# Hybrid decoder step on one core: partial sums of the second gated projection loaded with their gates, mixed forms in three places, and other numbers of staging places at the changes of passes

## The chip, the cores and the metric

The kernel runs on one core of a Trainium2 chip. The metric is the device time of one launch in microseconds (us). Three runs of the kernel before took 2620.25, 2620.29 and 2623.68 us; their median is 2620.29 us.

## The reference

One layer of a decoder is computed in float32 for 1024 prompt tokens and 8 sample tokens, 1032 columns in all, with a model width of 2048.

```
proj = rmsnorm(x, g_pre) @ w_in          # 2048 -> 10240: q k v za ub zb ga gb
ya   = (retention(q, k, v) * silu(za)) @ w_pa          # 1024 -> 2048
y    = gelu(s5(ub));  y = y * sigmoid(y @ w_glu + b)   # 1024 -> 1024
yb   = (y * silu(zb)) @ w_pb                           # 1024 -> 2048
merged = sigmoid(ga) * ya + sigmoid(gb) * yb
out    = x + rmsnorm(merged @ w_out, g_post)           # 2048 -> 2048
```

The states of the retention and of the S5 branch are outputs too; the change does not touch them.

## The kernel before

**Arithmetic.** Activations lie transposed: 128 features on the partitions, tokens along the free axis. Every float32 operand is split into a high and a low part (`whi`/`wlo` for weights, two halves of a tile for activations), and a product is three matmuls. The big projections go by a Winograd form of Strassen's scheme: two blocks of output rows and two halves of the columns are made from seven block products instead of eight. One *step* is one pair of output row blocks, and it has seven *products* n = 0 to 6, run by `product(g)` (L907), where g counts products through the whole program. Product n takes an activation *form* n, one of `FORMS = ("u1", "t2", "v1", "t3", "t1", "t4", "v2")` (L751): u1, v1 and v2 are plain quarters of the input, the t-forms are sums and differences of quarters. Four contraction blocks i = 0 to 3 make 28 form tiles for each pass.

**Passes.** After the passes over `w_in` come five more: `glu` (4 steps, from step SG), `pa` (8 steps, from SA), `pb` (8 steps, from SB), and `w_out` in two halves of its contraction, `o0` (8 steps, from SO) and `o1` (8 steps, from SP). In `o0` and `o1` the forms cover only columns 384 to 1031, 324 for each half; columns 0 to 383 are done last, in plain blocks (the matmuls of L1736), here called the *last stage*. `pa` is the first gated projection: its output times the gate `sga_d` is written to `pap_d` as a partial sum. `pb` is the second: its output times `sgb_d`, plus `pap_d`, is `merged`, written to `mg_d`, which `o0`, `o1` and the last stage read.

**What sets the order.** The code is written as one loop over products; each product is followed by its evacuation (`evac_p` L1453, `evac_o` L1549), by actions put at a product number with `at(g, ...)` (run by `late_work`, L1281), and by one `slot()` (L172) that runs a background generator up to its next `yield`. A scheduler then orders each engine's instructions, and may move a load ahead of where it is written. The engines run their own lists strictly in order. A DMA that an engine issues stands in that engine's list: if it has to wait (for data, or for a buffer), all that is behind it on that engine waits too. SyncE loads weights into `wr`; `prep(g + 2)` (L880) makes the weight tile of a product two products ahead: sums `wraw` on VectorE, then `whi` on ScalarE, then `wlo` on VectorE.

**Evacuation in `pb`.** ScalarE copies product 0 to a tile `p`; VectorE makes `u` tiles and the four results `st` (product 2), `u` (4), `p` (5), `u` (6), and multiplies each by its gate `zz`, which ScalarE's queue loaded two products before (`load_z`, L1423). Then `gated` (L1429) has GpSimd issue a DMA that adds `pap_d` into the tile in SBUF (L1450), and `LAG` = 4 products later a DMA that stores the tile to `mg_d` (L1451). There are two buffers of each kind of tile, one in use by this step and one by the step before.

**Change of passes.** `transition` (L1301) fills the forms of the next pass while the last two steps of the present pass run. With q the number of products since two steps before the new pass, it issues two loads `stg` at q = 0, 1, 2 and 3 (8 places, `stg_open(8)`), and from q = 3 to 19 it splits forms (`unstage`, L859: ScalarE's cast at L259, VectorE's difference), one for each product up to q = 6 and then two, and issues one more load into each place set free. So the four tiles of form n are split by q = 6 + 2n, and product n of the new pass is q = 14 + n.

**Mixed forms for `w_out`.** `forms_o(kh, wait)` (L1480) makes the t-forms of `o0` (from SB + 4) and of `o1` (from SO): for i = 0 to 3 it loads two row blocks of `mg_d`, does four VectorE operations in place, and stores both tiles to `fo_d`. It has two pairs of tiles, so the loads of i = 2 and 3 wait until the stores of i = 0 and 1 have landed.

**The last stage.** `load_m` and `split_m` (L1528, L1531) bring columns 0 to 383 of `mg_d`, four row blocks ahead. A row of `g_post`, spread over all partitions (1 MB, L1702), and the first block of x (1 MB, L1703) are loaded by GpSimd's queue right after the last product of `o1` in the text; `evac_c` (L1705) uses them at the end of each quarter of the last stage.

Of the kernel before, what the change touches and what calls it, by code (L numbers as in the profile page):

```python
# [18 lines left out]
D = 2048  # L19
# [60 lines left out]
def emit(ctx, tc, I, O):  # L80
# [854 lines left out]
    def at(g, f):  # L935
        due.setdefault(g, []).append(f)
# [360 lines left out]

    def stg_open(bufs):
        opened["stg"], opened["stgp"] = popen("stg3", "left", bufs)

    def transition(g, base, kind, eng=P):  # L1301

        q = g - 7 * base
        n = moved.setdefault(kind, [0, 0])
# [5 lines left out]
        if 0 <= q < 4:  # L1310
            load(eng)
            load(eng)
# [110 lines left out]
    def load_z(s, name):  # L1423
        kind, p = steps[s]
        r, c = AT[name]
        zq[name] = zz_tile()
        A.dma_start(zq[name], {"glu": zy_d, "pa": sga_d, "pb": sgb_d}[kind][2 * p + r, :, HT * c:HT * c + HT])

    def gated(g, name, t, ps=None):  # L1429
# [17 lines left out]
        if kind == "pa":  # L1447
            P.dma_start(pap_d[m, :, cols], t)
        else:
            P.dma_start(t, pap_d[m, :, cols], accum_op=ALU.add)  # L1450
            at(g + LAG, lambda: P.dma_start(mg_d[m, :, cols], t))  # L1451
# [28 lines left out]
    def forms_o(kh, wait):  # L1480
# [3 lines left out]
        def ld(i):  # L1484
            if i < 2:
                w[i] = act.tile([128, 2, TOK], F32, name=f"a{(6, 4)[kh] + i}")
            t[i] = w[i % 2][:, 0, 0:SW], w[i % 2][:, 1, 0:SW]
            for x, k in zip(t[i], (8 * kh + i, 8 * kh + 4 + i)):
                P.dma_start(x, mg_d[k, :, TA:TOK])

        for i in range(4):
            if i % 2 == 0:
                if i:
                    yield
                ld(i)
                if i:
                    yield
                ld(i + 1)
                for _ in range(wait):
                    yield  # L1500
            u, v = t.pop(i)
# [7 lines left out]
            P.dma_start(fo_d[kh, 1, i], v)  # L1509
            yield  # L1510

    flat_ = {}
# [15 lines left out]
    def load_m(m):  # L1528
        P.dma_start(spare(m), mg_d[m, :, 0:TA])
# [126 lines left out]
    for s in range(SG, len(steps)):  # L1656
# [3 lines left out]
        if s == SA + 1:  # L1660
            fx_open()
            bg.append(make_forms(yb_d, fb_d))
        if s == SB + 4:
            bg.append(forms_o(0, 2))
        if s in (SG + 2, SB - 2, SB + 6, SP - 2):
            drain()
            stg_open(8)
        if s == SO:
            zstack.close()
            bg.append(forms_o(1, 3))  # L1670
        if s == SO + 1:
# [6 lines left out]
        for n in range(7):  # L1678
# [15 lines left out]
            if s == len(steps) - 1:  # L1694
                for m in range(4) if not n else (n - 1,):
                    at(g, lambda m=m, n=n: split_m(m) if n else load_m(m))
            late_work(g)
# [3 lines left out]
    gb = flat(1, "gb")[:, 0:D]  # L1701
    P.dma_start(gb, bass.AP(tensor=I["g_post_row"].tensor, offset=I["g_post_row"].offset, ap=[[0, 128], [1, D]]))  # L1702
    P.dma_start(x_of(0), I["xB"][0])  # L1703

# [19 lines left out]
    for g in range(4):  # L1724
# [4 lines left out]
        for st in todo_:  # L1729
            for k, c in st:  # L1730
# [6 lines left out]
                if k == KD - 1:  # L1737
                    evac_c(g, c, ps[c])
            now[0] += 1
            if rest:  # L1740
                with ExitStack() as after:
# [87 lines left out]
```

## Time and profile before

| what | value |
|---|---|
| median of three runs | 2620.29 us |
| the profiled execution's own time | 2619.01 us |
| its span, first to last instruction | 2617.1 us |
| TensorE (PE) busy | 2565.9 us, 98% |
| VectorE (DVE), ScalarE (ACT), GpSimd (POOL) busy | 1983.2, 971.5, 784.4 us |
| `pb` ends, `o0` begins | 2249.70 us |
| `o1` ends, the last stage begins | 2466.16 us |

PE is the engine that is nearly always busy, so what counts is where it is not, and where its matmuls run slower than elsewhere. An "x" count in a table by stage is the number of instructions that touch the stage; with one kind of matmul it tells how much of the work got done in it. In rows of waits, "A <- B: total, times, longest" says that A stood idle until B released it. PEclk is the granted clock of TensorE as a share of full speed.

### The profile page before, as it was taken

The page shows a single profiled execution, that of the slowest core. Times are in us where ns is not written, and L with a number is a line of the kernel's source. Part 1 is how long each engine was busy: PE and PEld are TensorE (multiplying, and loading weights), DVE is VectorE, ACT ScalarE, POOL GpSimd, SP SyncE. Part 2 cuts the span into 40 slices and gives each one's busy share as a digit, 9 for nine tenths or more (in the row PEclk, how much of TensorE's full clock was granted, in tenths as well). Part 3 has the DMA queues.
Part 4 walks back from the last instruction along what each step waited for, and adds up shares of the span by engine and source line. Part 5 has one row for each costly group of instructions (what it writes and reads, how often), then busy time and mean ns, then how long its engine had stood idle before and what let it go on. Part 6 is the DMA issues. An engine that isn't in the chain of part 4 may idle for free.

```text
span 2617.1 us, 52507 instructions
## 1 busy us (share of the span) xinstructions
PE 2565.9 (98%) x19948; PEld 2518.0 (96%) x19948; DVE 1983.2 (76%) x4159; ACT 971.5 (37%) x1747; POOL 784.4 (30%) x1300
## 2 busy tenths in 40 slices
PE   9999999999999999999999999999999998799998
PEld 8999999999999999999999999999999998799976
DVE  6655988889889877558877766668886866788875
ACT  6113233333323324343333444346532422345532
POOL 0103322222222222333244444335221323523320
PEclk9999999999999999999999999999999999999999
DMA  5886434434444447888879888889786879957784
GB/s 192 265 267 209 151 115 127 138 119 120 133 122 128 131 138 236 205 208 198 201 200 247 228 205 227 203 207 298 248 275 236 249 197 249 275 174 175 196 303 139
DMA packets 233500, 519.09 MB, mean 198 GB/s; under 512 B 33968, under 2 KB 61056, under 8 KB 232480
## 3 DMA queue, kind: packets, MB, share of 16 engines
q0 software_dynamic: 106464, 308.09, 42.9%
q1 hardware_dynamic: 91552, 159.30, 19.8%
q10 hardware_dynamic: 35232, 48.36, 5.9%
q8 instruction: 157, 2.57, 0.4%
q14 instruction: 95, 0.78, 0.1%
HBM read 342.36 MB, written 173.25 MB: 197 GB/s over the span
## 4 chain that ended last, share of the span: by engine, by line
PE 81%; issue 6%; DMA 6%; DVE 3%; POOL 3%; ACT 1%; POOLq 0%; DVEq 0%; ACTq 0%; SPq 0%
PE acc L919 63%; PE acc L1736 5%; PE mm L214 2%; PE mm L212 2%; PE mm L213 2%; DMA u<-pap_d 1%; DMA fo_d<-a 1%; DVE a L85 1%; DMA a<-mg_d 1%; DMA st<-pap_d 1%; PE misc L637 1%; PE misc L715 1%; PE misc L714 1%; DVE wlo L85 1%; PE misc L1133 1%
## 5 line engine op out<-in xcount | busy, mean ns | idle before, releaser
L919 PE MATMUL acc<-a,whi 128*128 128x258 f32 (+1 forms) x10976 | 1844.0, 287 | 30.9 <-DVE u L85 22.3
L919 PEld LDWEIGHTS acc<-a,whi 128*128 128x128 f32 x10976 | 1545.2, 190 | 39.3 <-ACT whi L900 12.2
L919 PE MATMUL acc<-a,wlo 128*128 128x258 f32 (+1 forms) x5488 | 1156.8, 285 | 0.5 <-DVE wlo L85 0.5
L919 PEld LDWEIGHTS acc<-a,wlo 128*128 128x128 f32 x5488 | 866.9, 190 | 1.0 <-DVE wlo L85 1.0
L900 ACT CAST whi<-wraw 128x512 fp32r<-128x512 f32 x424 | 263.2, 621 | 690.0 <-PE acc L919 512.4
L85 DVE TENSOR_TENSOR wlo<-wraw,whi 128x512 fp32r<-128x512 f32 x456 | 312.7, 686 | 173.3 <-ACT whi L900 114.2
L900 ACT CAST whi<-wr 128x512 fp32r<-128x512 f32 x318 | 197.3, 621 | 567.3 <-PE acc L919 511.1
L85 DVE TENSOR_TENSOR wlo<-wr,whi 128x512 fp32r<-128x512 f32 x380 | 260.7, 686 | 72.7 <-ACT whi L900 41.7
L212 PE MATMUL mm<-a,whi 128*128 128x384 f32 (+1 forms) x448 | 145.1, 326 | 5.6 <-ACT whi L205 5.6
L85 DVE TENSOR_TENSOR wraw<-wr 128x512 f32<-128x512 f32 x212 | 145.5, 686 | 2.7
L213 PE MATMUL mm<-a,whi 128*128 128x384 f32 (+1 forms) x448 | 145.2, 324 | 0.1
L214 PE MATMUL mm<-a,wlo 128*128 128x384 f32 (+1 forms) x448 | 144.8, 323 | 0.1
L85 DVE TENSOR_TENSOR a<-stg,a 128x516 fp32r<-128x516 f32 (+1 forms) x196 | 118.0, 632 | 32.2 <-ACT a L259 27.9
L259 ACT CAST a<-stg 128x516 fp32r<-128x516 f32 (+1 forms) x196 | 104.8, 574 | 48.5 <-DMA stg<-mg_d 17.8
L1736 PE MATMUL acc<-whi,a 128*128 128x512 f32 x372 | 117.8, 395 | 1.9 <-ACT whi L205 1.9
L85 DVE TENSOR_TENSOR u<-acc,p 128x516 f32<-128x516 f32 (+1 forms) x106 | 70.1, 661 | 57.3 <-PE acc L919 56.7
L85 DVE TENSOR_TENSOR u<-acc,u 128x516 f32<-128x516 f32 (+1 forms) x100 | 67.3, 673 | 58.7 <-PE acc L919 57.7
L85 DVE TENSOR_TENSOR p<-acc,p 128x516 f32<-128x516 f32 (+1 forms) x100 | 67.2, 672 | 53.3 <-PE acc L919 53.2
L973 POOL DMA_DIRECT2D u<-pt_d x70 | 61.6, 881 | 117.7 <-DVE u L85 79.5
L85 DVE TENSOR_TENSOR u<-p,acc 128x516 f32<-128x516 f32 (+1 forms) x106 | 69.7, 657 | 32.5 <-PE acc L919 12.9
L971 POOL DMA_DIRECT2D pt_d<-u x70 | 38.6, 552 | 179.7 <-DVE u L85 129.7
L212 PEld LDWEIGHTS mm<-a,whi 128*128 128x128 f32 x448 | 84.5, 189 | 5.8 <-ACT whi L205 5.6
(395 smaller groups left out, 3080.8 us busy)
## 6 DMA issues: line engine op xcount, KB each, us to landing
wr<-in_w_in SPq DMA_DIRECT2D x280, 256.0 KB
pt_d<-u POOLq DMA_DIRECT2D x70, 258.0 KB, 3.1
u<-pt_d POOLq DMA_DIRECT2D x70, 258.0 KB, 5.0
wr<-in_w_out SPq DMA_DIRECT2D x64, 256.0 KB
wr<-in_w_outB SPq DMA_DIRECT2D x64, 256.0 KB
stg<-fm_d POOLq DMA_DIRECT2D x44, 258.0 KB, 4.4
pt_d<-st POOLq DMA_DIRECT2D x35, 258.0 KB, 3.2
pt_d<-p POOLq DMA_DIRECT2D x35, 258.0 KB, 3.1
```

The source lines that it names most:

```text
L85: return (eng or V).tensor_tensor(out, a, b, op)
L212: T.matmul(ps, wh[:, i, :], xh[:, t0:t1], start=first, stop=False)
L213: T.matmul(ps, wh[:, i, :], xl[:, t0:t1], start=False, stop=False)
L214: anchor["p"] = T.matmul(ps, wl[:, i, :], xh[:, t0:t1], start=False, stop=last).ins
L259: A.copy(dst[0], src)
L637: T.matmul(ps[0:16, g * 128:(g + 1) * 128], B1[:, g, :], W3[:, g, 0:8, :], start=True, stop=True)
L714: T.matmul(o, Tm[:, g, :], U[:, g, 0:136], start=True, stop=False)
L900: anchor["a"] = A.copy(hi, f).ins
L919: anchor["p"] = T.matmul(o, a[:, i, :], x, start=first and i == 0 and a is wh and b is xh, stop=n in (2, 5, 6) and i == 3 and a is wl, ski ...
L971: P.dma_start(pt, t)
L973: P.dma_start(t, pt, accum_op=ALU.add)
L1736: anchor["p"] = T.matmul(ps[c], a, b, start=k == 0 and a is xh and b is wh, stop=k == KD - 1 and a is xl).ins
```

## The change

There are four parts.

1. In `pb` from its third step on (p > 1), `load_z` also loads the piece of `pap_d` into a tile `pp` (a new pool of four) on ScalarE's queue, right behind the gate. `gated` then adds it with a VectorE operation and has GpSimd store the tile to `mg_d` at once. The adding DMA and the lag of four products are gone for these 24 tiles; the first two steps keep them. The pool `pp` stands from SB + 1 to SO + 1.
2. `forms_o` has three pairs of places in the same two tiles: the loads of i = 0, 1 and 2 do not wait for a store; i = 3 takes the place of i = 0. The waits written as `yield` change with it.
3. The number of staging places differs by pass: 6 instead of 8 for `o0` and 11 instead of 8 for `o1`; `transition` issues two loads for each product until all places are filled.
4. For the last stage, `load_m` of the first four blocks is written a little earlier, and the two loads of 1 MB are written into the last stage, after 9 and after 20 of its pieces.

```
@@ -1296,20 +1296,24 @@
         opened["fx"], opened["fxp"] = popen("fx", "left", 4)
 
     def stg_open(bufs):
+        opened["n"] = bufs
         opened["stg"], opened["stgp"] = popen("stg3", "left", bufs)
 
     def transition(g, base, kind, eng=P):
 
         q = g - 7 * base
-        n = moved.setdefault(kind, [0, 0])
+        n = moved.setdefault(kind, [0, 0, 0])
 
         def load(eng=P):
             at(g, lambda o=order_q[n[0]]: stage(opened["stgp"], kind, *o, eng))
             n[0] += 1
 
-        if 0 <= q < 4:
-            load(eng)
-            load(eng)
+        if q == 0:
+            n[2] = opened["n"]
+        for _ in range(2):
+            if 0 <= q and n[2]:
+                n[2] -= 1
+                load(eng)
         if 3 <= q < 20:
             for i in range(1 if q < 7 else 2):
                 if n[1] < 28:
@@ -1425,6 +1429,9 @@
         r, c = AT[name]
         zq[name] = zz_tile()
         A.dma_start(zq[name], {"glu": zy_d, "pa": sga_d, "pb": sgb_d}[kind][2 * p + r, :, HT * c:HT * c + HT])
+        if kind == "pb" and p > 1:
+            zq[name, "p"] = ppp.tile([128, HT], F32, name="pp")
+            A.dma_start(zq[name, "p"], pap_d[2 * p + r, :, HT * c:HT * c + HT])
 
     def gated(g, name, t, ps=None):
         s = g // 7
@@ -1446,6 +1453,9 @@
             mul(two(t), ps, two(z))
         if kind == "pa":
             P.dma_start(pap_d[m, :, cols], t)
+        elif (name, "p") in zq:
+            add(t, t, zq.pop((name, "p")))
+            P.dma_start(mg_d[m, :, cols], t)
         else:
             P.dma_start(t, pap_d[m, :, cols], accum_op=ALU.add)
             at(g + LAG, lambda: P.dma_start(mg_d[m, :, cols], t))
@@ -1482,22 +1492,21 @@
         t, w = {}, {}
 
         def ld(i):
-            if i < 2:
-                w[i] = act.tile([128, 2, TOK], F32, name=f"a{(6, 4)[kh] + i}")
-            t[i] = w[i % 2][:, 0, 0:SW], w[i % 2][:, 1, 0:SW]
+            a, b = w[0], w[1]
+            t[i] = {0: a[0:2], 1: b[0:2], 2: (a[2], b[2]), 3: a[0:2]}[i]
             for x, k in zip(t[i], (8 * kh + i, 8 * kh + 4 + i)):
                 P.dma_start(x, mg_d[k, :, TA:TOK])
 
+        for j in range(2):
+            f = act.tile([128, 4 * HT], F32, name=f"a{(6, 4)[kh] + j}")
+            w[j] = [f[:, SW * i:SW * i + SW] for i in range(3)]
+        ld(0)
+        ld(1)
+        for n in range(wait):
+            yield
+            if n == 1:
+                ld(2)
         for i in range(4):
-            if i % 2 == 0:
-                if i:
-                    yield
-                ld(i)
-                if i:
-                    yield
-                ld(i + 1)
-                for _ in range(wait):
-                    yield
             u, v = t.pop(i)
             u1, u2, v1, v2 = u[:, 0:HO], u[:, HO:SW], v[:, 0:HO], v[:, HO:SW]
             sub(u1, u1, u2)
@@ -1508,6 +1517,10 @@
             P.dma_start(fo_d[kh, 0, i], u)
             P.dma_start(fo_d[kh, 1, i], v)
             yield
+            if i == 1:
+                ld(3)
+                for _ in range(wait - 3):
+                    yield
 
     flat_ = {}
 
@@ -1660,14 +1673,18 @@
         if s == SA + 1:
             fx_open()
             bg.append(make_forms(yb_d, fb_d))
+        if s == SB + 1:
+            ppstack, ppp = popen("pp", "left", 4)
+        if s == SO + 1:
+            ppstack.close()
         if s == SB + 4:
-            bg.append(forms_o(0, 2))
+            bg.append(forms_o(0, 3))
         if s in (SG + 2, SB - 2, SB + 6, SP - 2):
             drain()
-            stg_open(8)
+            stg_open({SB + 6: 6, SP - 2: 11}.get(s, 8))
         if s == SO:
             zstack.close()
-            bg.append(forms_o(1, 3))
+            bg.append(forms_o(1, 6))
         if s == SO + 1:
             zrstack, zr0 = popen("zr", "left", 4)
             zrp = [zr0]
@@ -1692,15 +1709,15 @@
                 raw_of["pool"] = wst
                 next_w()
             if s == len(steps) - 1:
-                for m in range(4) if not n else (n - 1,):
-                    at(g, lambda m=m, n=n: split_m(m) if n else load_m(m))
+                if n:
+                    at(g, lambda m=n - 1: split_m(m))
+            if s == len(steps) - 2 and n > 2:
+                at(g, lambda m=n - 3: load_m(m))
             late_work(g)
             slot()
     small = const.tile([128, 24], F32, name="small")
     sm = [(small[:, o:o + 4], small[:, o + 4:o + 5], small[:, o + 5:o + 6], small[:, o + 6:o + 7]) for o in (0, 8, 16)]
     gb = flat(1, "gb")[:, 0:D]
-    P.dma_start(gb, bass.AP(tensor=I["g_post_row"].tensor, offset=I["g_post_row"].offset, ap=[[0, 128], [1, D]]))
-    P.dma_start(x_of(0), I["xB"][0])
 
     def evac_c(g, c, ps):
         s4, r1, r2, r3 = sm[c]
@@ -1737,6 +1754,10 @@
                 if k == KD - 1:
                     evac_c(g, c, ps[c])
             now[0] += 1
+            if now[0] == lim[0] + 9:
+                P.dma_start(gb, bass.AP(tensor=I["g_post_row"].tensor, offset=I["g_post_row"].offset, ap=[[0, 128], [1, D]]))
+            if now[0] == lim[0] + 20:
+                P.dma_start(x_of(0), I["xB"][0])
             if rest:
                 with ExitStack() as after:
                     for ins in anchor.values():
```

How the instructions stand now is shown at three places. The first is GpSimd's list in the third step of `pb` (p = 2), where the four results are `st`, `u`, `p` and `u`; before:

```order
L1450 DMA st<-pap_d 128x516
L1451 DMA mg_d<-st 128x516
L1450 DMA u_26948<-pap_d 128x516
L1451 DMA mg_d<-u_26948 128x516
L1450 DMA p_26840<-pap_d 128x516
L1450 DMA u_26883<-pap_d 128x516
L1451 DMA mg_d<-p_26840 128x516
L1451 DMA mg_d<-u_26883 128x516
```

and now, with loads of `forms_o` (L1498) among them:

```order
L1458 DMA mg_d<-st 128x516
L1458 DMA mg_d<-u_26956 128x516
L1458 DMA mg_d<-p_26843 128x516
L1498 DMA a_27359<-mg_d 128x648
L1458 DMA mg_d<-u_26888 128x516
L1498 DMA a_27358<-mg_d 128x648
```

The four adding loads are gone from the list, and each store stands where the adding load stood.

The second place is GpSimd's list in the last two steps of `pb`, where the places for `o0` are filled again; before, from the first result of step SB + 6:

```order
L1450 DMA st<-pap_d 128x516
L857 DMA stg<-mg_d 128x324
L1451 DMA mg_d<-st 128x516
L857 DMA stg<-mg_d 128x324
L1450 DMA u_27977<-pap_d 128x516
L857 DMA stg<-mg_d 128x324
L1451 DMA mg_d<-u_27977 128x516
L1450 DMA p_27857<-pap_d 128x516
L857 DMA stg<-mg_d 128x324
L1450 DMA u_27904<-pap_d 128x516
L857 DMA stg<-fo_d 128x324 x2
```

and now, from the store of the same result:

```order
L1458 DMA mg_d<-st 128x516
L857 DMA stg<-fo_d 128x324 x2
L857 DMA stg<-mg_d 128x324
L1458 DMA mg_d<-u_28018 128x516
L857 DMA stg<-mg_d 128x324
L1458 DMA mg_d<-p_27895 128x516
L1458 DMA mg_d<-u_27944 128x516
L857 DMA stg<-mg_d 128x324 x2
L857 DMA stg<-fo_d 128x324 x4
```

Before, eight forms were loaded ahead of this and the ones shown begin with v1; now six were, so that two of t2 come first. Between two loads stands at most a store, and no adding load.

The third place is GpSimd's list at the begin of the last stage (`a<-mg_d` are loads of `load_m`, `<-pt_d` the adding loads of `o1`'s results); before:

```order
L1703 DMA a_31037<-in_xB 128x2048
L1559 DMA p_30877<-pt_d 128x324
L1559 DMA u_30904<-pt_d 128x324
L1529 DMA a_29823<-mg_d 128x384
L1702 DMA a_31035<-in_g_post_row 128x2048
L1529 DMA a_29986<-mg_d 128x384 x2
L1529 DMA a_29823<-mg_d 128x384 x2
```

and now:

```order
L1760 DMA a_31546<-in_xB 128x2048
L1572 DMA p_30933<-pt_d 128x324
L1572 DMA u_30956<-pt_d 128x324
L1542 DMA a_29875<-mg_d 128x384
L1542 DMA a_30038<-mg_d 128x384 x2
L1542 DMA a_29875<-mg_d 128x384
L1758 DMA a_31087<-in_g_post_row 128x2048
```

The scheduler has put the load of x back where it was; the row of `g_post` has moved behind three loads of `load_m`.

More of the change, by code (lines that the diff above doesn't have):

```diff
@@ L1308, in load @@
             n[0] += 1
-        if 0 <= q < 4:
-            load(eng)
-            load(eng)
+        if q == 0:
+            n[2] = opened["n"]
+        for _ in range(2):
+            if 0 <= q and n[2]:
+                n[2] -= 1
+                load(eng)
         if 3 <= q < 20:
@@ L1510, in forms_o @@
             yield
+            if i == 1:
+                ld(3)
+                for _ in range(wait - 3):
+                    yield
     flat_ = {}
@@ L1694, in emit @@
             if s == len(steps) - 1:
[L1695 to L1696 removed]
+                if n:
+                    at(g, lambda m=n - 1: split_m(m))
+            if s == len(steps) - 2 and n > 2:
+                at(g, lambda m=n - 3: load_m(m))
             late_work(g)
```

48 lines of the change are left out of this document (30 added, 18 removed).

## The prediction

> **What bounds the kernel now.** I read the page first, then tables by stage, then PE's timeline and the waits where a stage lost time.
>
> ```profile
> PE 2565.9 (98%) x19948; PEld 2518.0 (96%) x19948; DVE 1983.2 (76%) x4159; ACT 971.5 (37%) x1747; POOL 784.4 (30%) x1300
> ```
>
> PE has hardly any idle time as an average, so what is to be had lies where a stage got less done than its neighbours. This table of PE by stage has the stage, its length, busy time with the count of matmuls, the granted clock, the DMA share and GB/s:
>
> ```profile
> 2000.00:2140.00 140.00, 140.00 (x1169) 1.00 0.74 216
> 2140.00:2249.70 109.70, 89.89 (x686) 0.92 0.87 232
> 2249.70:2300.00 50.30, 42.08 (x264) 0.97 0.91 293
> 2300.00:2340.00 40.00, 40.00 (x271) 1.00 0.44 148
> 2340.00:2466.16 126.16, 123.80 (x816) 0.99 0.71 169
> 2466.16:2604.60 138.44, 136.21 (x595) 1.00 0.70 230
> ```
>
> Undisturbed, a matmul of the gated passes takes 140/1169 = 0.1198 us, one of `o0` and `o1` 40/271 = 0.1476 us. So the second half of `pb` (2140 to 2249.7) needed 686 x 0.1198 = 82.2 us and took 109.7: **27.5 us lost**. The begin of `o0` needed 264 x 0.1476 = 39.0 of 50.3: **11.3 lost**. The rest to the last stage needed 816 x 0.1476 = 120.4 of 126.2: **5.7 lost**. The busy column hides part of this, because matmuls behind a stall are slow:
>
> ```profile
> 2372.44 0.31 PE L919 MATMUL acc<-a,wlo 128*128 128x324 f32 x1
> 2374.27 0.56 PE L919 MATMUL acc<-a,whi 128*128 128x324 f32 x2 [1.52 <-ACT whi L900]
> 2376.16 0.74 PE L919 MATMUL acc<-a,whi 128*128 128x324 f32 x2
> 2379.17 0.46 PE L919 MATMUL acc<-a,whi 128*128 128x324 f32 x2
> 2478.63 0.50 PE L1736 MATMUL acc<-whi,a 128*128 128x512 f32 x1 [1.94 <-ACT whi L205]
> ```
>
> A pair takes 0.74 us instead of 0.46 until about 2378.6, so a stall of 1.5 us costs nearly 2 us on top. The Trainium skill, "TensorE: Matmul & The Clock Gate" (Part 1), says that the clock drops to half after an idle window of about 3.4 us; by it a short stall would cost only itself. The trace has the drop after 1.52 us, and the measurement decides. The last stage lost the 1.9 us of its stall. Together 27.5 + 11.3 + 5.7 + 1.9 = **46.4 us** lie within reach of the change; the rest of the kernel it doesn't touch.
>
> Who makes PE wait in `pb`, from the waits of 2140 to 2249.7:
>
> ```profile
> POOL mg_d L1451 <- DMA u<-pap_d: 24.3, 10, 5.8
> POOL mg_d L1451 <- DMA p<-pap_d: 16.2, 5, 4.2
> DVE a L85 <- DMA a<-mg_d: 15.8, 4, 5.2
> PE acc L919 <- DVE u L85: 15.1, 5, 7.5
> POOL mg_d L1451 <- DMA st<-pap_d: 15.0, 4, 4.9
> ACT a L259 <- DMA stg<-mg_d: 13.8, 4, 5.7
> ACT p L1457 <- DMA mg_d<-p: 8.4, 3, 5.5
> PE acc L919 <- ACT p L1457: 3.7, 1, 3.7
> ```
>
> POOL is the root: it stands 24.3 + 16.2 + 15.0 = 55.5 of 109.7 us before a store, until an adding load has landed. Behind it in its list wait the loads of mixed forms (for which DVE waits 15.8 us) and staged forms (for which ACT waits 13.8), and stores come so late that ACT waits 8.4 us for the tile `p`. Each of these engines works in order, so the weights' casts and the evacuation come late and PE waits.
>
> **Part 1, the sums.** Gone: 24 adding loads, and all 55.5 us of waiting but that for what is left of the first two steps, done before 2140. Added on ACT: 24 issues; on DVE: 24 additions. Their prices:
>
> ```profile
> 2240.70 0.33 ACTq L1427 DMA_DIRECT2D zz<-sgb_d x1
> ...
> 2250.34 0.68 DVE L85 TENSOR_TENSOR wlo<-wraw,whi 128x512 fp32r<-128x512 f32 x1
> 2250.95 0.68 DVE L85 TENSOR_TENSOR p<-p,zz 128x516 f32<-128x516 f32 x1
> 2251.55 0.89 DVE L85 TENSOR_TENSOR a<-stg,a 128x324 fp32r<-128x324 f32 x2
> 2252.36 0.69 DVE L85 TENSOR_TENSOR u<-acc,u 128x516 f32<-128x516 f32 x1
> ```
>
> 24 x 0.33 = 8 us on ACT; from start to start an addition of this size takes 0.605 us, so 24 x 0.605 = 14.5 us on DVE; a split of 324 columns takes 0.405. The cover is PE's time:
>
> ```profile
> 2060.00:2080.00 20.00, 20.00 (x169) 20.00 (x169) 20.00 (x34) 10.08 (x18) 6.51 (x11) 1.00 0.78 234
> 2080.00:2100.00 20.00, 20.00 (x169) 20.00 (x168) 12.88 (x21) 4.84 (x8) 5.34 (x9) 1.00 0.84 229
> ```
>
> (Here the columns are PE, PEld, DVE, ACT, POOL.) A plain step of `pb` is 7 x 24 matmuls, 20.1 us, with DVE busy 12.9 and ACT 4.8. It becomes 12.9 + 4 x 0.605 = 15.3 and 4.8 + 4 x 0.33 = 6.1, both covered. In the last step of `pb`, 14 splits of `o0` add 5.7: 15.3 + 5.7 = 21 against 20.1, or 20.2 by start-to-start times (24 x 0.605 + 14 x 0.405). DVE is then full, as in the row of 2060 to 2080, where PE lost nothing. If the cover were gone, each step would cost the difference. I take 0 (bounds 0 and 4 us) and book what is left of `pb`'s 27.5 as 1 us.
>
> Who waits newly: POOL's store for DVE's addition, within a product's time; DVE for `pp`. It is issued right behind the gate, two products (5.7 us) before its use, and PE still has weights for two products then. The waits list no wait of DVE for a gate.
>
> **Part 2, the mixed forms.** DVE's 15.8 us of waits are for i = 2 and 3, loaded after stores had landed. Now only i = 3 waits for a landing, with two mixings (four slots) in between. I book 0 and let this part go with part 1: its loss is in the 27.5.
>
> **Part 3, the places.** For `o0` there are 6 places for 8. A place set free by the split of form tile k takes tile k + 6, which is needed three products later instead of four: 8.6 us in `pb`, but 3 x 12 x 0.1476 = 5.3 us once `o0` runs. Landings:
>
> ```profile
> zz<-sgb_d ACTq DMA_DIRECT2D x16, 258.0 KB
> fo_d<-a POOLq DMA_DIRECT2D x8, 324.0 KB, 6.0
> u<-pap_d POOLq DMA_DIRECT2D x9, 258.0 KB, 6.2
> stg<-fo_d POOLq DMA_DIRECT2D x12, 162.0 KB, 5.6
> ```
>
> 5.6 us from issue to landing and 0.5 for the issue are more than 5.3, so ACT will wait 1 to 2 us there, two or three times; PE's lead of two products (3.5 us) should take most of it. Now 11.3 us are lost, since the loads stood behind adding loads. Bounds: 0 left, or all 11.3. I take **4 left**: one stall of 1.5 to 2 us and its slow matmuls. For `o1` the 11 places bring the last loads forward:
>
> ```profile
> 2371.45 0.91 ACT L259 CAST a<-stg 128x324 fp32r<-128x324 f32 x2 [2.70 <-DMA stg<-mg_d]
> 2371.94 0.95 DVE L85 TENSOR_TENSOR a<-stg,a 128x324 fp32r<-128x324 f32 x2 [1.67 <-ACT a L259]
> ```
>
> This wait holds up the weights that PE misses at 2374.27, and it should go. What is late next is DVE, with two splits of 0.405 for each product; it was nearly full here already (third column):
>
> ```profile
> 2340.00:2360.00 20.00, 20.00 (x136) 20.00 (x135) 19.34 (x39) 13.48 (x30) 9.77 (x19) 1.00 0.71 218
> ```
>
> Bounds 0 to 5.7; I take **2 left**.
>
> **Part 4, the last stage.** The order shows the load of x where it was; only the row of `g_post` comes behind three loads.
>
> ```profile
> 2465.33 0.56 POOL L1703 DMA_DIRECT2D a<-in_xB  x1
> 2468.74 0.86 POOL L1702 DMA_DIRECT2D a<-in_g_post_row  x1
> 2477.54 0.51 ACT L259 CAST a<-a 128x384 fp32r<-128x384 f32 x1 [5.03 <-DMA a<-mg_d]
> ```
>
> ACT's wait of 5.0 us is for a load issued among these two of 1 MB. One of them goes, and the 1.9 us should halve: **1 left** (bounds 0 and 1.9). `g_post` is used first near the end of the first quarter (138.44/4 = 34.6 us long), so it isn't late.
>
> **The sum.** 1 + 4 + 2 + 1 = 8 us are left of 46.4, so 38.4 are saved. The profiled execution took 2619.01 us by its own time (1.9 more than its span); the median of the runs is 1.28 above it. 2619.01 - 38.4 = 2580.6, and for the median 2581.9. The floor, with nothing left, is 2573.9.
>
> **The rivals.** *The change of passes stays bound.* Six places are too few and DVE is full from the last step of `pb` to the sixth product of `o0`. Against it: the two passes before changed with DVE full and no loss. `o0` and `o1` would lose what they do now: 2581.9 + (11.3 - 4) + (5.7 - 2) = 2592.9.
>
> *The DMA engines bound it.* From 2140 to 2300 the core moved 109.7 x 232 + 50.3 x 293 = 40.2 MB. PE alone needs 121.2 us for that work, so 332 GB/s would be wanted.
>
> ```profile
> 1900.00:1980.00 80.00, 80.00 (x669) 80.00 (x669) 66.88 (x108) 24.69 (x43) 22.04 (x42) 1.00 0.87 296
> ```
>
> This is the fastest long stretch with PE full that resembles it. At 296 GB/s the bytes take 135.8 us, a loss of 14.6 where I book 5: 2581.9 + 9.6 = 2591.5. Against it: part of the bytes can be moved earlier or later than this window. The Trainium skill, "Trainium Kernel Development and Optimization", says that DMAs of SP, ACT and POOL run on the same 16 engines, so that issuing from several saves only issue time. By that rule moving the partial sums to ACT's queue takes no byte away, which is this rival; the trace, where POOL waits for single landings of 6 us at a DMA share of 0.87, speaks for latency.
>
> *POOL stays the root.* The loads of mixed forms still wait for stores to land (6.0 us each), and stores of results stand behind them. Half of 27.5 stays: 2581.9 + 13 = 2595.
>
> *Slower.* `pp` lands late. DVE stands before 24 additions, and all its later work (weights too) waits. It decides from a landing of about 5.7 + 3.5 = 9 us, the lead of the load and a cautious lead of PE's weights. At 12 us each addition costs 3 us: 24 x 3 = 72, 2654. For it: 258 KB more on a queue that shares busy DMA engines. Against it: 6.2 us was the median of the slower, adding form. *Nothing*: a chain that I don't see replaces POOL's, and 2620 stays.
>
> **How the numbers follow.** Forecast (2574 to 2590) 0.58; the change of passes 0.14; DMA 0.14; POOL 0.07; nothing 0.03; slower 0.04. The range runs from the floor, 2573, up over the first two rivals and the third with some room, 2600. Faster by over 0.2% (5 us, about what a measurement here can tell): 0.58 + 0.14 + 0.14 + 0.07 = 0.93; within 0.2%: 0.03; slower: 0.04.
>
> **What would show it.** Right: from the third step of `pb` to `o0`, PE at 0.120 us a matmul with no gap over 1 us; POOL's waits before `mg_d` on VectorE and no longer on DMA; DVE 15.3 us busy in a plain step of `pb`; a short gap in the first step of `o0` behind ACT's wait for `stg`. Wrong: DVE waiting for `pp`, granted clock below 1 in the middle of `pb`, or a DMA share near 1 through the whole second half of `pb` with PE idle.

## The result and the profile after

| | before | after |
|---|---|---|
| median, us | 2620.27 (2616.25 to 2623.68, 4 runs) | 2580.95 (2579.69 to 2582.84, 4 runs) |
| ratio after/before | | 0.9851, 95% interval 0.9834 to 0.9868 |
| profiled execution, us | 2619.01 | 2581.53 |
| from the first matmul of `product` to `o0` | 2009.12 | 1981.49 |
| `o0` to the last stage | 216.46 | 206.07 |
| last stage to the last matmul's end | 140.27 | 139.97 |

The prediction said 2581.9 us; the median is 2580.95. The three last rows of the table come from the begins of the matmuls in the two traces. They are counted from the first matmul that `product` issues, since what comes before it takes some tenths of a us more or less in each execution. 27.6 us went before `o0` begins, 10.4 between `o0` and the last stage, 0.3 in the last stage, 38.3 in all. The two profiled executions differ by 37.5; what lies outside these stages took 0.8 more.

The first lines of the page after:

```profile
PE 2555.1 (99%) x19948; PEld 2509.8 (97%) x19948; DVE 1997.5 (77%) x4183; ACT 971.1 (38%) x1747; POOL 761.7 (30%) x1276
```

PE did the same 19948 matmuls. DVE has 24 instructions more and 14.3 us more of work; POOL has 24 fewer. The table of PE by stage, with the same columns as before the change and cut at the same places of the program:

```profile
2000.00:2140.00 140.00, 140.00 (x1169) 1.00 0.76 234
2140.66:2222.71 82.05, 82.05 (x686) 1.00 0.91 299
2222.71:2273.01 50.30, 48.21 (x311) 0.97 0.88 288
2273.01:2313.00 39.99, 39.99 (x271) 1.00 0.45 148
2313.00:2428.78 115.78, 114.94 (x769) 1.00 0.74 171
2428.78:2568.80 140.02, 138.00 (x602) 1.00 0.70 233
```

The second half of `pb` holds the same 686 matmuls and takes 82.05 us instead of 109.70: at 0.1196 us a matmul nothing is lost in it. The begin of `o0` got 311 matmuls done in 50.30 us instead of 264; 50.30 - 311 x 0.1476 = 4.4 us are still lost. The rest to the last stage lost 115.78 - 769 x 0.1476 = 2.3, the last stage about 1.9 by its idle time.

The longest waits of POOL in 2140.66 to 2222.71 (the total, how often, the longest one), and the only one of VectorE there that has to do with a store:

```profile
POOL stg L857 <- DVE a L85: 13.3, 8, 2.3
POOL a L1498 <- DMA mg_d<-u: 10.9, 2, 5.6
POOL mg_d L1458 <- DVE st L85: 9.4, 3, 7.4
POOL mg_d L1458 <- DVE u L85: 8.1, 4, 3.1
...
DVE st L85 <- DMA mg_d<-p: 0.8, 1, 0.8
```

POOL still stands, but before its stores it waits for VectorE's addition and not for a landing. PE waits for nothing in this stretch, and VectorE stands only 0.8 us behind a store. What is left of PE's stalls after that is in these rows of PE's timeline (start, length, what ran, and in brackets the idle time before it and its releaser):

```profile
2233.81 0.54 PE L919 MATMUL acc<-a,whi 128*128 128x324 f32 x2 [1.87 <-DVE u L85]
2235.38 0.74 PE L919 MATMUL acc<-a,whi 128*128 128x324 f32 x2
2238.63 0.46 PE L919 MATMUL acc<-a,whi 128*128 128x324 f32 x2
...
2339.32 0.42 PE L919 MATMUL acc<-a,wlo 128*128 128x324 f32 x1 [0.31 <-DVE wlo L85]
...
2440.99 0.50 PE L1753 MATMUL acc<-whi,a 128*128 128x512 f32 x1 [1.68 <-ACT whi L205]
```

One stall in `o0` of 1.87 us, with pairs of 0.74 us instead of 0.46 for about 4 us behind it; nothing over 0.5 us in the change to `o1`; one stall of 1.68 us in the last stage.

### The profile page after: what moved, and what is told of

Its sections match the earlier page's. It is cut to its first block, busy times and chain, and to the rows that moved or that the text cites. A ratio compares the mean times of both kernels' runs of the same rounds, so it can differ in the third digit from the quotient of the medians.

```text
span 2579.5 us, 52551 instructions
## 1 busy us (share of the span) xinstructions
PE 2555.1 (99%) x19948; PEld 2509.8 (97%) x19948; DVE 1997.5 (77%) x4183; ACT 971.1 (38%) x1747; POOL 761.7 (30%) x1276
## 4 chain that ended last, share of the span: by engine, by line
PE 91%; DVE 3%; issue 2%; DMA 2%; ACT 1%; POOL 1%; DVEq 0%; POOLq 0%; ACTq 0%
PE acc L919 73%; PE acc L1753 5%; PE mm L214 3%; PE mm L212 3%; PE mm L213 2%; DVE a L85 1%; DMA xr<-in_xT 1%; PE misc L637 1%; PE misc L715 1%; PE misc L714 1%; PE misc L1133 1%; PE misc L1123 1%; PE misc L1102 1%; DMA a<-mg_d 1%; PE misc L665 1%
```

## The experiments

The theory: GpSimd's list was the root, because the store behind each adding load waits in order until that load has landed, and all loads of forms stand behind it. The rivals: the bytes and the DMA engines bound that stretch; the loads of mixed forms and places were what mattered; the additions on VectorE or the new loads have a price that is hidden or not. The table has all runs; the three columns of stages are from the profiled executions and are cut as above. Each ratio is to executions of the kernel before in the same comparison. Where neither a range nor a ratio is given there was one execution.

| run | median, us | ratio to before, 95% interval | to `o0` | `o0` to last stage | last stage |
|---|---|---|---|---|---|
| before | 2620.27 | 1 | 2009.12 | 216.46 | 140.27 |
| after | 2580.95 | 0.9851, 0.9834 to 0.9868 | 1981.49 | 206.07 | 139.97 |
| part 1 alone | 2585.51 (2582.84 to 2587.42) | 0.9869, 0.9847 to 0.9891 | 1981.46 | 209.06 | 141.48 |
| all but part 1 | 2617.65 (2614.30 to 2622.89) | 0.9995, 0.9985 to 1.0006 | 2013.49 | 209.84 | 140.09 |
| all but part 2 | 2584.66 (2583.19 to 2586.27) | 0.9866, 0.9849 to 0.9884 | 1981.48 | 207.69 | 142.56 |
| before, stores by SyncE | 2586.91 (2583.72 to 2589.55) | 0.9874, 0.9856 to 0.9893 | 1981.53 | 211.05 | 142.87 |
| 8 places for `o0` | 2579.91 (2578.31 to 2580.32) | 0.9847, 0.9833 to 0.9860 | 1981.48 | 202.93 | 142.20 |
| 8 places and late loads | 2577.04 (2576.07 to 2578.19) | 0.9838, 0.9824 to 0.9851 | 1981.47 | 202.99 | 138.45 |
| late loads | 2578.60 | | 1981.47 | 205.80 | 137.98 |
| 8 places for `o1` | 2582.94 | | 1981.58 | 206.09 | 142.05 |
| all but part 4 | 2583.70 | | 1981.45 | 205.02 | 143.90 |
| added twice | 2586.47 | | 1981.48 | 209.22 | 142.87 |
| `pp` by GpSimd | 2588.97 | | 1985.87 | 206.18 | 143.89 |

The last stage differs by some 4 us even between kernels whose edits don't touch it (see the last section), so a single time is judged here by the stage that its edit touches.

### Part 1 alone

The kernel before with the loads of `pp` and the additions. The change's 6 places for `o0` come with it, since the pool `pp` takes the room of two.

```
+        if kind == "pb" and p > 1:
+            zq[name, "p"] = ppp.tile([128, HT], F32, name="pp")
+            A.dma_start(zq[name, "p"], pap_d[...])
...
+        elif (name, "p") in zq:
+            add(t, t, zq.pop((name, "p")))
+            P.dma_start(mg_d[m, :, cols], t)
```

> Part 1 alone: the partial sums are loaded with the gates and added on VectorE; the mixed forms, the last stage and the 8 places of o1 are as before, and o0 has 6 places, since pp takes the room. Theory (GpSimd's waits for adding loads are the root): the second half of pb loses 0 to 3 of its 27.5 us, o0 loses 4 to 7, o1 as before about 5.7; time 2583 to 2588. Rival (the mixed forms' third place is what frees VectorE, 15.8 us of waits): half of pb's loss or more stays; time 2594 to 2602.

Measured: 1981.46 us to `o0`, the same as with the whole change, and 209.06 from there on against 216.46 before and 206.07 after. So all of the gain in `pb` and 7.4 of the 10.4 us behind it come with part 1 and its 6 places. The other parts bring 3.0 us there on top, and 4.6 by the medians.

### All but part 1

The whole change without `pp`: adding loads, the lag of four products, and 8 places for `o0`, as before. The load of i = 2 stands one slot later than in the change.

```
-        if kind == "pb" and p > 1:
-            zq[name, "p"] = ppp.tile([128, HT], F32, name="pp")
-            A.dma_start(zq[name, "p"], pap_d[...])
...
-            stg_open({SB + 6: 6, SP - 2: 11}.get(s, 8))
+            stg_open({SP - 2: 11}.get(s, 8))
```

> The change without part 1: third place for mixed forms (the load of i = 2 one slot later, since the stores keep their lag), 8 places for o0, 11 for o1, the last stage as changed. Theory: GpSimd still stands before every store of pb, so pb loses 20 us or more and o0 8 or more; only o1 gains, 2 to 4 us; time 2608 to 2618. Rival (mixed forms): pb loses under 14 us; time 2596 to 2606.

PE in the second half of `pb` and at the begin of `o0`, by stage:

```profile
2140.00:2254.02 114.02, 91.79 (x687) 0.90 0.83 220
2254.02:2304.30 50.28, 44.49 (x286) 0.97 0.93 299
```

and the longest waits of 2140 to 2254:

```profile
POOL mg_d L1455 <- DMA u<-pap_d: 26.0, 9, 5.9
DVE a L85 <- DMA a<-mg_d: 18.1, 3, 9.5
PE acc L919 <- DVE u L85: 18.0, 3, 7.2
POOL mg_d L1455 <- DMA p<-pap_d: 16.3, 5, 4.7
POOL mg_d L1455 <- DMA st<-pap_d: 13.6, 4, 4.6
```

POOL stands before its stores for 26.0 + 16.3 + 13.6 = 55.9 us, as it did before the change (55.5). VectorE waits for the loads of mixed forms even longer than before, 18.1 us, although three pairs of places no longer wait for a store. `pb` gets 4.4 us longer, the passes behind it 6.6 shorter (3.2 at the begin of `o0`, 3.2 at the change to `o1` with its 11 places), and the whole doesn't differ measurably from before. The rival that has the places of the mixed forms as the cause of the loss in `pb` falls.

### All but part 2

The change with the mixed forms as they were, two pairs of places.

```
-            t[i] = {0: a[0:2], 1: b[0:2], 2: (a[2], b[2]), 3: a[0:2]}[i]
+            if i < 2:
+                w[i] = act.tile([128, 2, TOK], F32, name=f"a{(6, 4)[kh] + i}")
+            t[i] = w[i % 2][:, 0, 0:SW], w[i % 2][:, 1, 0:SW]
```

> The change without part 2: the mixed forms have two places as before. Theory: without adding loads the loads of mixed forms are no longer late in GpSimd's list, so VectorE's waits for them shrink to 1 to 4 us each and PE's lead takes them; pb loses 0 to 3 us; time 2580 to 2585. Rival: pb loses 8 us or more; time 2589 or more.

PE at the begin of `o0`:

```profile
2222.99:2273.29 50.30, 46.05 (x301) 1.00 0.85 285
```

Measured: nothing in `pb` (1981.48), and 207.69 against 206.07 us from `o0` on. At the begin of `o0` 50.30 - 301 x 0.1476 = 5.9 us are lost instead of 4.4, so the third pair of places is worth about 1.5 us against the profile after, and nearly all of it there. The scatter has to be set beside that: five profiles with this stage as in the change (after, 8 places for `o1`, late loads, all but part 4, `pp` by GpSimd) lost 3.1 to 4.5 us in it. The two with two pairs of places and 6 staging places, this one and part 1 alone, lost 5.9 and 6.0, and both have a second stall of 1.8 us some 19 us into `o0` that none of the five has. So the gain is real, 1.4 to 2.9 us. The two profiled executions differ by 4.5 us, but 2.6 of that lies in the last stage, which this part doesn't touch.

### Before, with the stores of `pb` issued by SyncE

This tells the two main theories apart: the adding loads stay, with all their bytes and the lag, and only the store that waits for them stands in another engine's list.

```
-            at(g + LAG, lambda: P.dma_start(mg_d[m, :, cols], t))
+            at(g + LAG, lambda: nc.sync.dma_start(mg_d[m, :, cols], t))
```

> The kernel before with one thing changed: the store of each pb result (lag of four products kept) is issued by SyncE instead of GpSimd, so that GpSimd no longer stands waiting for an adding load to land. Bytes, adding loads and tiles are as before. Theory (the in-order wait on GpSimd is the root, not the adding loads themselves nor DMA bytes): most of pb's and a good part of o0's loss goes, 15 to 33 of 38.8 us; time 2587 to 2605; what stays is SyncE's weights behind its new waits. Rival (DMA engines bound it, or the adding load's own 6 us): little goes, 0 to 8 us; time 2612 to 2621.

PE by stage in the second half of `pb`:

```profile
2140.60:2222.69 82.09, 82.09 (x687) 1.00 1.01 294
```

and SyncE's waits in it:

```profile
SPq L1451 <- DMA st<-pap_d: 22.5, 5, 8.3
SPq L1451 <- DMA u<-pap_d: 21.8, 7, 7.8
SPq L1451 <- DMA p<-pap_d: 19.6, 4, 6.0
```

All of the 27.6 us before `o0` are gone with one word changed, and 5.1 of the 11.3 lost at the begin of `o0`. The waits for the landings are all there, 22.5 + 21.8 + 19.6 = 63.9 us, and harm nobody, because SyncE had slack in its list. In the kernel before it stood more than that there waiting for weight buffers:

```profile
SPq L876 <- DVE wraw L85: 70.5, 8, 12.2
SPq L876 <- DVE wlo L85: 31.4, 8, 11.2
```

The DMA share is 1.01 at 294 GB/s and PE is full all the same, so the rival of the bytes falls for `pb`. That part 1 adds anything to this kernel isn't shown. The medians of the two, 2586.91 here and 2585.51 with part 1 alone, have overlapping ranges, and the 2.0 us between their passes behind `pb` (211.05 and 209.06) lie at the change to `o1`, where both have 8 places: 5.6 us are lost here against 3.8, since slow matmuls (0.74 us a pair) followed the stall here and not there.

### 8 places for `o0`

In the whole change; the pool `pp` gets three tiles instead of four to make room.

```
-            ppstack, ppp = popen("pp", "left", 4)
+            ppstack, ppp = popen("pp", "left", 3)
...
-            stg_open({SB + 6: 6, SP - 2: 11}.get(s, 8))
+            stg_open({SB + 6: 8, SP - 2: 11}.get(s, 8))
```

> The changed kernel with 8 places for o0 instead of 6; the room comes from pp, which has three tiles instead of four. Theory (the 4.4 us that o0 still loses come from the short time for a load once o0 runs: three products instead of four): the stall of 1.9 us and its slow matmuls go, o0 to last stage takes 202 to 204 us instead of 206.1; time 2577 to 2580. Rival (VectorE, full from the last step of pb on, is what is late there): the stall stays at over 1 us, 205.5 to 206.5; time as the changed kernel, 2580 to 2582.

ScalarE's casts in the first products of `o0`, in the kernel after the change:

```profile
2227.05 0.47 ACT L259 CAST a<-stg 128x324 fp32r<-128x324 f32 x1 [0.88 <-DMA stg<-fo_d]
...
2229.73 0.46 ACT L259 CAST a<-stg 128x324 fp32r<-128x324 f32 x1 [1.70 <-DMA stg<-fo_d]
...
2231.67 0.90 ACT L259 CAST a<-stg 128x324 fp32r<-128x324 f32 x2 [0.62 <-DMA stg<-fo_d]
```

These three waits add up to 3.2 us. VectorE, which makes the other half of each form, waits behind them:

```profile
2232.16 0.50 DVE L85 TENSOR_TENSOR a<-stg,a 128x324 fp32r<-128x324 f32 x1 [1.44 <-ACT a L259]
...
2233.18 0.49 DVE L85 TENSOR_TENSOR u<-acc,p 128x324 f32<-128x324 f32 x1
```

and the operation on `u` that comes behind it frees the accumulator for which PE stands 1.87 us until 2233.81. With 8 places, PE by stage at the begin of `o0`:

```profile
2222.05:2272.35 50.30, 49.77 (x332) 1.00 0.88 296
```

332 matmuls instead of 311 in the same 50.30 us, no drop of the granted clock, 50.30 - 332 x 0.1476 = 1.3 us lost instead of 4.4. ScalarE waits only once more, 1.30 us, and PE stands 0.31. From `o0` to the last stage it is 3.1 us less. The run with both edits below repeats this stage (332 matmuls, 1.3 us lost). The price of 6 places that the prediction had worked out (5.3 us of work per place against landings of 5.6) is thus shown for the change as it is. The median gained only 1.0 and lies within the spread of the last stage, which here took 2.2 us longer than in the profile after.

### 8 places for `o1`

```
-            stg_open({SB + 6: 6, SP - 2: 11}.get(s, 8))
+            stg_open({SB + 6: 6}.get(s, 8))
```

> The changed kernel with 8 places for o1 instead of 11. Theory: ScalarE waits again for the last loads of o1, PE has a stall of 1.2 to 1.8 us in the first step of o1 with its slow matmuls, and o0 to last stage takes 3 to 4 us more, 209 to 210; pb is as changed. Rival (o1's loss came from the same late GpSimd list as pb's): no stall over 0.5 us there, 206 to 206.5.

Two stages of PE, the begin of `o0` and what lies from the change to `o1` up to the last stage:

```profile
2221.93:2272.23 50.30, 48.27 (x320) 1.00 0.85 286
...
2312.23:2428.02 115.79, 114.00 (x759) 1.00 0.72 173
```

A miss: I had expected some 3 us more than after, and the sum is the same (206.09 against 206.07). From there 115.79 - 759 x 0.1476 = 3.8 us are lost against 2.3, so 11 places are worth about 1.5 us there. That was made up for by `o0`, which lost 1.3 us less without being touched: its stall of 1.48 us left the granted clock at 1.00, where the 1.87 us of the profile after were followed by slow matmuls. The stall that I had expected at the change to `o1` did come, 0.95 us long behind ScalarE's weights (2337.65), but without slow matmuls. All profiles together show what the places do. The four kernels with 8 places for `o1` have a stall of 0.95 to 1.52 us there; two lost 3.8 us (this one and part 1 alone), two lost 5.6 and 5.7 with slow matmuls behind the stall (stores by SyncE, before). The nine with 11 places have no stall over 0.31 us and lost 2.2 to 2.5.

### Late loads, alone and with 8 places for `o0`

The change writes the loads of x and `g_post` into the last stage, but the scheduler put the load of x back to its begin. A VectorE copy of one column from a weight tile of that moment into the target holds each load where it is written.

```
             if now[0] == lim[0] + 9:
+                V.tensor_copy(gb[:, 0:1], wb[g, k][1][:, 0:1].bitcast(F32))
                 P.dma_start(gb, ...)
             if now[0] == lim[0] + 20:
+                V.tensor_copy(x_of(0)[:, 0:1], wb[g, k][1][:, 0:1].bitcast(F32))
                 P.dma_start(x_of(0), I["xB"][0])
```

> The changed kernel with only the two loads of 1 MB really moved into the last stage, in the same way. Theory: the stall at the begin of the last stage, 1.7 us, goes or shrinks under 0.7; o0 is as in the changed kernel (a stall of about 1.9). Rival: the stall stays at over 1 us.

> As the run with 8 places for o0, and the two loads of 1 MB really moved into the last stage: a VectorE copy of one column of a weight tile into each destination makes the load wait for that weight. Theory: the loads of the last stage's first blocks then land in time, its stall of 1.7 + 0.2 us goes; time 2575 to 2579. Rival (these loads are late because of the adding loads of o1's last results and the weights): the stall stays at over 1 us and nothing is gained over 8 places alone.

In the kernel after the change, the two loads on GpSimd and ScalarE's first long wait of the last stage:

```profile
2427.95 0.55 POOL L1760 DMA_DIRECT2D a<-in_xB  x1
...
2433.85 0.54 POOL L1758 DMA_DIRECT2D a<-in_g_post_row  x1
...
2439.91 0.51 ACT L259 CAST a<-a 128x384 fp32r<-128x384 f32 x1 [5.84 <-DMA a<-mg_d]
```

With both edits:

```profile
2428.70 0.51 ACT L259 CAST a<-a 128x384 fp32r<-128x384 f32 x1 [0.78 <-DMA a<-mg_d]
...
2442.20 0.53 POOL L1759 DMA_DIRECT2D a<-in_g_post_row  x1 [6.07 <-PE acc L1753]
...
2469.08 0.54 POOL L1762 DMA_DIRECT2D a<-in_xB  x1
```

Counted from the begin of the stage, the load of x is issued 45 us later and the row of `g_post` 12 us later; ScalarE no longer waits 5.8 us for a block of `mg_d`, and PE's stall of 1.68 us is gone. The late loads alone bring the last stage to 137.98 us and leave `o0` as it was (205.80, with a stall of 1.85 us). Both edits together take 2577.04 us, 3.9 less than the change and 43.7 less than the kernel before by the medians of their own comparisons; the runs of this version (2576.07 to 2578.19) lie below all those of the change (2579.69 to 2582.84), though the two intervals of the ratio overlap. It is the best version of this study.

### All but part 4

```
+    P.dma_start(gb, ...)
+    P.dma_start(x_of(0), I["xB"][0])
...
-            if now[0] == lim[0] + 9:
-                P.dma_start(gb, ...)
-            if now[0] == lim[0] + 20:
-                P.dma_start(x_of(0), I["xB"][0])
```

and the four `load_m` after the last product of `o1`, as before.

> The changed kernel without part 4: first loads of the last stage's blocks and the two loads of 1 MB as before. Theory: the scheduler had moved most of it back, so only the row of g_post comes two or three loads earlier: the stall at the begin of the last stage is 1.7 to 2.4 us (1.7 in the changed kernel), all else as changed; time 2580 to 2584. Rival (part 4 saves 1 us or more): stall and slow matmuls cost 1 us or more beyond the changed kernel's last stage of 140.0 us.

Measured: 143.90 us in the last stage, 3.9 more than after, with a stall of 3.14 us, longer than I had expected (1.7 to 2.4), and slow matmuls behind it. But other runs that have part 4 as it is show the same (143.89 with `pp` by GpSimd, 142.87 with the sums added twice), and the kernel before took 140.27 without it. What part 4 brings as it is written isn't resolved by this; at 1.9 us of loss both before and after I can't show that it brought anything.

### Added twice

Doubles VectorE's price of part 1: after each addition a second one of the same size writes into the spent `pp` tile, whose value nobody reads.

```
-            add(t, t, zq.pop((name, "p")))
+            pp_ = zq.pop((name, "p"))
+            add(t, t, pp_)
+            add(pp_, t, pp_)
```

> The changed kernel with each of the 24 additions on VectorE followed by a second one of the same size into the spent pp tile (its result is not used), so that the cost of an addition without cover shows. VectorE has 24 x 0.605 = 14.5 us more, four for each step of pb. Theory: 15.3 + 2.4 = 17.7 of 20.1 us in a plain step, still covered; in the last step of pb 22.6 of 20.1, so that VectorE falls 2 to 3 us behind there: main loop to o0 takes 1981 to 1983 us, and o0 loses 1 to 4 us more than in the changed kernel. Rival (the additions already cost time in every step): 24 x 0.6 = 10 us or more on pb, 1990 or more.

Measured: `pb` isn't harmed at all (1981.48 us), and `o0` to the last stage takes 3.15 more. The cover in `pb` holds 24 further additions, 14.5 us of VectorE. What it doesn't hold is the change to `o0`, where VectorE was full with one addition already.

### `pp` loaded by GpSimd

The rival that would have made the change slower: VectorE waits for `pp`. Here the load stands in the list that part 1 had relieved.

```
-            A.dma_start(zq[name, "p"], pap_d[...])
+            P.dma_start(zq[name, "p"], pap_d[...])
```

> The changed kernel with pp loaded by GpSimd's queue instead of ScalarE's: 24 more issues of 0.55 us on GpSimd, none of which has to wait for a landing. Theory (waiting in the list, not the number of issues or the kind of queue, makes the loss): pb loses 0 to 1 us, main loop to o0 takes 1981.5 to 1982.5; o0 up to 2 us more, since its loads stand behind more issues. Rival (the gain is from the other kind of queue): 1990 or more.

The one place where time was lost, in the fourth step of `pb`: GpSimd, VectorE and PE.

```profile
2117.26 0.56 POOL L1461 DMA_DIRECT2D mg_d<-u  x1 [6.08 <-DMA u<-pap_d]
...
2131.10 0.54 POOL L1434 DMA_DIRECT2D pp<-pap_d  x1
...
2136.95 0.70 DVE L85 TENSOR_TENSOR st<-st,pp 128x516 f32<-128x516 f32 x1 [5.16 <-DMA pp<-pap_d]
...
2138.39 1.20 PE L919 MATMUL acc<-a,whi 128*128 128x258 f32 x4 [2.58 <-DVE u L85]
```

1985.87 us, 4.4 more than after, lies between what either theory had said (at most 1982.5, at least 1990). The stores of the first two steps still wait for their adding loads (6.08 us here). The four tiles of `pp` for the third step had been loaded before that, at 2078.8 to 2080.9; the first one for the fourth step is issued late, VectorE stands 5.16 us and PE 2.58 and is slow behind it. Once the last adding load is through, no later step loses anything. The mechanism of the rival is real, but it needs the in-order wait ahead of it in the same list; with ScalarE's list it didn't come up in a single one of the 24 additions.

## Why the prediction was right

**`pb`: 27.5 us to be had, 1 left.** Nothing is left (686 matmuls in 82.05 us). The root is shown by the run with SyncE's stores, in which only the place of the waiting store differs. The rival of the DMA engines had its own sign, a share near 1 with PE idle; the share came to 0.91 at 299 GB/s in the change and 1.01 in that run, with PE full both times. Its mistake was to take the fastest stretch of the trace of before, 296 GB/s at 0.87, for a ceiling, where PE already took all it could use; in the last stage after, 35 us with PE full moved 340 GB/s (2462.78 to 2497.78). Bytes also moved ahead, as the prediction had held against this rival: 2000 to 2140 carried 234 GB/s instead of 216.

**The cover for the additions.** VectorE in a plain step and in the last step of `pb`, after (PE, PEld, DVE, ACT, POOL):

```profile
2110.00:2130.00 20.00, 20.00 (x169) 20.00 (x168) 15.74 (x24) 4.84 (x8) 5.64 (x10) 1.00 0.82 236
...
2202.60:2222.70 20.10, 20.10 (x169) 20.10 (x169) 19.91 (x37) 10.37 (x23) 9.73 (x19) 1.00 0.93 298
```

I had worked out 15.3 and 20.2 to 21 of 20.1; it is 15.7 and 19.9, and PE lost nothing. Price 0, as booked. That it is 0 because of slack in `pb` alone, and no longer so in `o0`, is what the second addition shows.

**`o0`: 4 left.** 4.4, by the way that was given: ScalarE short of staged forms, one stall of 1.87 us, slow matmuls behind it. 8 places take it away. That the size fits so well is partly luck: in the two profiles of the same stage whose stall no slow matmuls followed, 3.1 and 3.4 us were lost.

**`o1`: 2 left.** 2.3. The stall of 1.52 us is gone; its largest follow-up is 0.31 us behind VectorE's `wlo`, which was named as what is late next.

**The last stage: 1 left.** This step failed, by 1 us. "One of them goes, and the 1.9 us should halve": one of the two loads did go behind, and ScalarE's wait became 5.84 us instead of 5.03, the loss stayed 1.9. So it wasn't enough to put the row of `g_post` behind three loads. The stall goes when both loads are held back; that it is the load of x at the begin of the stage that delays the blocks of `mg_d` is likely, but no run holds back one of them alone.

**Part 2: 0.** Right for `pb`, where a run without it is the same to 0.01 us; 1.4 to 2.9 us too low for the begin of `o0`. How these loads act on it was not tried apart. The 4 us for `o0` were worked out from the staging places alone, and they came out with a part in place that was booked at nothing; without it 5.9 were lost.

**The rival "slower".** It was held to be unlikely because 6.2 us were "the median of the slower, adding form". The plain loads of `pp` on GpSimd's queue took 6.6 us in the median, up to 10.1, so that reason doesn't hold. After the change `pp` was issued some 10 us ahead of its use (2102.0 for an addition at 2111.8) and not 5.7, and none of the 24 additions waited for it.

In all 8 us were to be left, and 0 + 4.4 + 2.3 + 1.9 = 8.6 are, of 46.4 that were counted in the trace of before. The sum is nearer than its terms: 1 too much for `pb` stands against 0.4, 0.3 and 0.9 too little for the others. That the median lies within 1 us of the forecast is luck in part, too. The profiled execution took 0.9 us more than the 2580.6 of the prediction, and the median then lay 0.6 below the profiled execution and not 1.28 above it. The slow matmuls behind a short stall, which the prediction took from the trace, came up again: 1.87 us of idle time were followed by them in `o0`.

## What to carry to other kernels

Here a DMA that depended on another DMA's landing held up everything behind it in its engine's list for the whole latency, and it cost time in the second half of `pb`, where the loads of forms stood behind it. In 2000 to 2140 of the kernel before GpSimd stood 31.8 us before such stores, and PE lost nothing. So find the in-order list that stands, and move the dependent transfer to a list with slack, or load ahead and let an engine with cover do the addition. The number of staging places that was enough here followed from the landing time against the time in which a place's neighbours are consumed, at the pace of the pass that consumes them and not of the one that loads. And look up in the order where the scheduler has put a load that was "moved"; here a copy that makes a true dependence kept it in its place.

## What the runs showed of the hardware

A stall of about the same length sometimes costs only itself and sometimes a slow stretch. At the begin of the last stage, without part 2, a stall of 1.59 us was followed by slow matmuls:

```profile
2442.81 0.49 PE L1750 MATMUL acc<-whi,a 128*128 128x512 f32 x1 [1.59 <-ACT whi L205]
...
2443.99 1.06 PE L1750 MATMUL acc<-whi,a 128*128 128x512 f32 x2
```

With part 1 alone, at the same place, a stall of 2.10 us was not:

```profile
2443.44 0.49 PE L1750 MATMUL acc<-whi,a 128*128 128x512 f32 x1 [2.10 <-ACT whi L205]
...
2444.50 0.62 PE L1750 MATMUL acc<-whi,a 128*128 128x512 f32 x2
```

The granted clock over the first 34 us of the stage was 0.95 in the first case and 1.00 in the second. At the begin of `o0` it was the same: slow matmuls followed stalls of 1.36 (with another of 0.31 behind it), 1.85, 1.87 and 2.02 us (`pp` by GpSimd, late loads, after, added twice), and none followed stalls of 1.48, 1.73 and 2.10 us (8 places for `o1`, all but part 4, stores by SyncE). So the length of a stall between 1.4 and 2.1 us doesn't tell which it will be; what decides it stays open.

The stall at its begin and the slow matmuls behind it make up most of what the last stage varies by. These are its first 34 us after the change (a stall of 1.68 us), then without part 4 (3.14 us), then with both of the best version's edits (no stall):

```profile
2428.78:2462.78 34.00, 32.03 (x148) 1.00 0.85 273
```

```profile
2426.87:2460.87 34.00, 30.80 (x131) 0.90 0.79 251
```

```profile
2424.99:2458.99 34.00, 33.93 (x158) 1.00 0.85 258
```

148, 131 and 158 matmuls in the same time: this stretch holds nearly all of the 138 to 144 us over which the last stage spread. The Trainium skill, "TensorE: Matmul & The Clock Gate" (Part 1), has the clock drop after an idle window of about 3.4 us. Here it also dropped after shorter stalls, down to 1.4 us, and not always.

A mean busy share of the DMA engines of 1.01, at 294 GB/s, went with a PE that never waited (stores by SyncE, 2140.60 to 2222.69), so that share alone was no sign of a bound.
